# Adaptive-vector matmuls behind the first gate block, their weights in other buffers, and the sample's attention woven into two latent tiles

## The chip, the cores and the metric

One core of one Trainium2 chip runs the whole kernel in one launch. The metric is the device time of that launch in microseconds (us). The engines are named as the profile names them: PE (TensorE, matmuls; PEld is its weight load), DVE (VectorE), ACT (ScalarE), POOL (GpSimd) and SP (SyncE). SP and POOL issue nearly all DMAs.

## The reference, cut to what matters

One layer of a streaming encoder is computed for a prompt of 1024 rows and for a sample of 32 rows with 512 rows of cache; both share the weights. The model width is 1024.

```python
ada = jax.nn.silu(c) @ w_ada + b_ada            # 6 vectors of 1024 for each of the two groups
sh1, sc1, gt1, sh2, sc2, gt2 = split(ada, 6)
h = rms_norm(x, g_pre_mix) * (1 + sc1) + sh1
p = h @ w_in                                     # q-latent, kv-latent, rope key, SB q, k, v, gate A, gate B
# branch B ("SB", stick-breaking, strictly causal, 8 heads of 64):
z = einsum('bqhd,bshd->bhqs', q, k) * 0.125
sp = where(mask, softplus(z), 0); later = reversed_cumsum(sp) - sp
o_B = einsum(where(mask, exp(log_sigmoid(z) - later), 0), v)
# branch A: latent attention with softmax, from rms_norm(q-latent) and rms_norm(kv-latent)
merged = sigmoid(gate A) * (o_A @ w_proj_a) + sigmoid(gate B) * (o_B @ w_proj_b)
```

For the sample, branch B runs over 512 cached keys and values (`cache_sb_k`, `cache_sb_v`) and the 32 new ones. A projection, an output matrix and a convolutional feed-forward part follow; the change does not touch them.

## The kernel before, in words

A float32 product is made of three matmuls on a high and a low part of each factor (`mm3`, lines 72 to 74): ACT makes the high part of a weight tile (`wh`, line 65) and DVE the low part (`wl`, line 68) from the raw tile `wr`. The raw tiles come from the pool `W`, which has two buffers under the tag `wr`.

The stages that matter run one after the other:

- `stage_h` makes `h` and needs the first two adaptive vectors; `stage_qkv` makes SB's q, k and v and spills them to DRAM.
- `stage_sb` is SB attention of the prompt in four pairs of heads. For each pair the order of PE, ACT and DVE is written out by hand in the string `ORDER`. A token is a step and a tile: `S` scores (PE, lines 1117 and 1118, into one of three `s` banks), `a e l` Abs, Exp, Ln (ACT), `x c d` the softplus, the reversed running sum and the exponent (DVE; `d` is line 739 and is the last reader of the score bank), `E` Exp (ACT), `T h v` transposes and their two parts (PE, ACT, DVE), `V` the product with the values (PE, line 796), `o p` the output.
- Between these tokens stands filler work for PE, the token `f`: one step of the generator `gates`, which makes the 16 column tiles of the two gates. A tile `m` is 26 steps: two of `ada_step` (line 216, small matmuls on one tile of `w_ada` each), which make a part of the adaptive vectors 3 to 6, and three blocks of columns (`BLK`, eight `mm3` steps each). Each block and each `ada_step` fills one of two `mm` banks. The token `G` is ACT's copy of a block out of its bank (line 1046) and a DMA to DRAM; `D` and `Q` are DVE's steps on the adaptive vector (`D` is line 226: it adds the bank onto the tile `ada`, which a DMA on POOL has filled from `b_ada`, line 224). `W` and `w` split the next gate tile's weights.
- After the fourth pair the sample's branch B follows (`sb_sample`, for two pairs of heads each, `b` = 1 and then 0): transposes of the cached keys (line 984), scores (993, 995), weights (`sb_weights`, lines 806 to 817), transposes of them (940, 943) and the product with the values (954, 957). `stage_lat` makes the two tiles of the kv-latent (m = 3, 4, called x and y below; three blocks of 24 matmuls each), their sum of squares (`lat_sums`, line 1142) and then the q-latent.

What sets the order around the change: in `stage_sb` the hand-written order on PE, ACT and DVE; elsewhere, and for SP and POOL, a scheduler that builds the queues. Each queue runs in order, and an instruction that waits holds up all behind it.

Before, the two `ada_step` steps stand at the head of each tile, ahead of block 0. Their weights use the pool `W`, the same two `wr` buffers as the gate weights; only the first two tiles have places of their own (`ada_first`, in the pool of `stage_sb`). `b_ada` is loaded onto the tile `ada` when the vector begins. The sample's q, k, v (`sbd`) and caches are loaded into the pool `att`, which is opened after `stage_sb`, and the sample's steps and latent tiles stand in blocks: x, then the first half of `b` = 1, y, and so on, as the scheduler puts them.

Of the kernel before, what the change touches and what calls it, by code (L numbers as in the profile page):

```python
# [17 lines left out]
P = 128  # L18
# [26 lines left out]
class K:  # L45
    def __init__(self, tc, a, ctx):
        self.tc, self.nc, self.a, self.ctx = tc, tc.nc, a, ctx
        self.n = 0
        self.in_w = []

# [6 lines left out]
    def tl(self, pool, shape, dt=F32, tag=None, bufs=None):  # L57
        return pool.tile(shape, dt, tag=tag, name=self.nm(tag or "t"), bufs=bufs or self.BUFS.get(tag))
# [17 lines left out]

    def wload(self, parts):

        nc = self.nc
        raw = self.tl(self.W, [P, 1024], F32, "wr")  # L80
        for c0, n, src, k in parts:
            nc.sync.dma_start(raw[:, c0 : c0 + n].rearrange("p (k c) -> p k c", k=k), src)
        return raw
# [99 lines left out]
    def ada_prep(self, tp):  # L183
# [16 lines left out]
        self.cT = self.cp.tile([P, 8, 32], F32, name="cT")  # L200
        nc.vector.memset(self.cT, 0.0)
        nc.vector.tensor_copy(self.cT[:, :, 0:2], ps[:, 0:16].rearrange("p (j k) -> p k j", j=2))
        self.gtd = self.dr.tile([2, 2, D], F32, name="gtd")
        self.ada_todo = [(v, k) for v in range(2, 6) for k in range(KT)]

    def ada_step(self, n, pool, tp, late):
# [13 lines left out]
        if self.ada_todo[0][1] == 0:  # L220
            self.acc = self.tl(tp, [P, 256], F32, "ada")
            for j in range(4):
                c = v * D + j * 256
                nc.gpsimd.dma_start(self.acc[32 * j : 32 * j + 32], a["b_ada"][0, c : c + 256].partition_broadcast(32))
        acc = self.acc
        late.append(lambda: nc.vector.tensor_tensor(acc, acc, ps[:, :256], ALU.add))
        del self.ada_todo[:n]
        self.ada_sum = v if k == KT - 1 else None
# [196 lines left out]
    def stage_qkv(self):  # L425
# [248 lines left out]
        S2.1a x2.0b G f1 a2.1a d1.1 e2.1a c2.0b f1 f1 E1.1 f1 w l2.1a S2.1b f1 a2.1b x2.1a T1.1 e2.1b T1.0 d2.0b  # L674
        h1.1 c2.1a f1 h1.0 f1 l2.1b v1.1 S3.0a E2.0b v1.0 f1 a3.0a f1 k2.1a d2.1a G e3.0a x2.1b V1.1 E2.1a c2.1b
        l3.0a S3.0b V1.0 x3.0a a3.0b o1 f1 p1 T2.2 h2.2 e3.0b d2.1b f1 c3.0a f1 E2.1b f1 l3.0b v2.2 S3.1a k3.0a
        d3.0a T2.1 h2.1 a3.1a x3.0b E3.0a V2.2 f1 D c3.0b T2.0 e3.1a S3.1b h2.0 f1 v2.1 l3.1a f1 v2.0 a3.1b f1
        x3.1a W f1 d3.0b V2.1 c3.1a G V2.0 f1 w o2 S4.0 e3.1b E3.0b f1 a4.0 f1 l3.1b f1 p2 e4.0 k3.1a d3.1a l4.0
# [3 lines left out]
        f1 o3 c5.1 f1 a6.0b l6.0a e6.0b f1 p3 l6.0b d5.1 f2 x6.0b E5.1 V4.0 x6.0a D f1 o4 c6.0a S6.1a T5.1 p4  # L682
        a6.1a T5.0 k6.0a d6.0a h5.1 f1 c6.0b e6.1a f1 h5.0 v5.1 f1 E6.0a v5.0 S6.1b l6.1a f1 W f1 x6.1a d6.0b
        V5.1 V5.0 G c6.1a E6.0b a6.1b S7.0a w o5 f1 f1 e6.1b l6.1b a7.0a f1 k6.1a p5 e7.0a f1 d6.1a x6.1b E6.1a
        f1 c6.1b l7.0a S7.0b f1 x7.0a T6.2 a7.0b f1 d6.1b h6.2 c7.0a f1 E6.1b f1 G e7.0b S7.1a v6.2 f1 k7.0a
        d7.0a l7.0b T6.1 T6.0 a7.1a h6.1 V6.2 x7.0b c7.0b h6.0 S7.1b e7.1a f1 v6.1 E7.0a f1 v6.0 l7.1a f1 d7.0b
        a7.1b f1 x7.1a V6.1 E7.0b V6.0 e7.1b c7.1a f1 G o6 l7.1b f1 p6 k7.1a d7.1a x7.1b f1 f1 E7.1a f1 D c7.1b
        f2 T7.3 d7.1b T7.2 h7.3 f1 h7.2 E7.1b v7.3 f1 f1 v7.2 f1 V7.3 V7.2 G Q T7.1 f1 h7.1 v7.1 T7.0 f1 h7.0
        v7.0 f1 V7.1 f2 V7.0 f1 o7 f1 W p7 f2 w G f7 G
# [269 lines left out]

    def sb_sample(self, b):  # L960

        nc, a = self.nc, self.a
        os = self.osb
# [6 lines left out]
        hs = slice(4 * b, 4 * b + 4)  # L970
        ck = self.tl(self.At, [P, TP], F32, "A")
        with self.tc.issue_after(self.fetched):
            nc.sync.dma_start(ck.rearrange("p (t c) -> p t c", t=4),
                          a["cache_sb_k"][0, 0, :, hs].rearrange("(t p) h d -> p t (h d)", p=P))
        cv = self.tl(self.At, [P, BIG], F32, "big")
        with self.tc.issue_after(self.fetched):
            nc.sync.dma_start(cv[:, :TP].rearrange("p (t c) -> p t c", t=4),
                          a["cache_sb_v"][0, 0, :, hs].rearrange("(t p) h d -> p t (h d)", p=P))
        mm = [self.tl(self.At, [P, TP], F32, "A") for _ in range(2)]
        for pp in range(2):  # L980
# [5 lines left out]
            nc.vector.tensor_copy(mm[pp][:, PAST:KS], self.ksb[:, 2 * b + pp])  # L986
        pieces = []
# [10 lines left out]
        B = self.sb_weights(pieces[::-1], KS)  # L998

# [5 lines left out]
        def rest():  # L1005
            self.pv_sample(self.ptrans_sample(B), b, vals, os)
            for k in (2 * b, 2 * b + 1):
                nc.gpsimd.dma_start(self.obd[k][:, TP:T], os[:, k])

        return rest  # L1010

    def gates(self):
# [59 lines left out]
    def stage_sb(self):  # L1072
# [61 lines left out]
        for r, c in self.SB:  # L1134
            nc.sync.dma_start(x[r, c], self.sbd[r, c])
# [1435 lines left out]
```

## Time and profile before

| | us |
|---|---|
| median of 3 runs | 1716.11 (1715.53 to 1716.94) |
| the profiled execution's own time | 1719.25 |
| its span, first to last instruction | 1716.4 |
| PE busy in the span | 1663.4 |
| DVE busy | 1272.2 |
| ACT busy | 994.1 |
| POOL busy | 297.0 |

The profile is of one execution. Times in it count from the span's start. `stage_sb` lies from about 192 to 517 us, the sample's branch B and the latent tiles from about 517 to 565 us. In the rows of the timeline the columns are start, duration, engine, line, operation, output and inputs, shape, number of instructions, and in brackets how long the engine had idled and what released it. The granted clock (PEclk) is the share of full clock that PE was given in a stretch.

### The profile page before, as it was taken

Reading aid. Unit: us, or ns where it says so; the run is one execution under the profiler, and the core shown is the slowest. Engines: PE = TensorE matmul, PEld = TensorE weight load, DVE = VectorE, ACT = ScalarE, POOL = GpSimd, SP = SyncE. Lnnn points to the kernel's source line nnn. Section 1 sums busy time; section 2 is a strip of 40 time slices with the busy share of each in tenths; the row PEclk is TensorE's granted clock in tenths of the full one; section 3 lists DMA queues with packets and bytes.
Section 4 is the critical chain, followed back from the end, with each engine's and each line's share of the span. In section 5 each row is a group of like instructions: output and inputs, shape, how many; then the busy total and the mean of one; then the engine's idle time right before and its main releaser. Section 6 shows DMA issues by size and latency. Waiting matters only on the chain. (4 is left out here: it accounts for less than half of the span.)

```text
span 1716.4 us, 30275 instructions
## 1 busy us (share of the span) xinstructions
PE 1663.4 (97%) x11646; PEld 1516.1 (88%) x11646; DVE 1272.2 (74%) x2129; ACT 994.1 (58%) x1945; POOL 297.0 (17%) x569
## 2 busy tenths in 40 slices
PE   5999799999998999999999999999999999999997
PEld 3999799999998899988889789999999999977885
DVE  4865497979793488887776779887777787788456
ACT  4544487978783567777773476544444444544442
POOL 2113312111110131111100121211111122110013
PEclk8999899999999999999999999999999999999999
DMA  9345855565533331222174531423333333697643
GB/s 328 112 127 186 298 153 166 168 176 158 162 112 103 118 97 53 68 66 73 60 275 144 177 124 61 142 93 130 132 103 131 131 106 133 236 331 244 215 138 119
DMA packets 185728, 255.20 MB, mean 149 GB/s; under 512 B 14702, under 2 KB 125056, under 8 KB 185584
## 3 DMA queue, kind: packets, MB, share of 16 engines
q1 hardware_dynamic: 164944, 194.11, 36.3%
q0 software_dynamic: 20416, 59.08, 9.8%
q8 instruction: 91, 1.49, 0.4%
q14 instruction: 53, 0.43, 0.1%
q10 hardware_dynamic: 224, 0.09, 0.0%
HBM read 187.86 MB, written 64.57 MB: 147 GB/s over the span
## 5 line engine op out<-in xcount | busy, mean ns | idle before, releaser
L65 ACT ACTIVATE wh<-wr 128x1024 fp32r<-128x1024 f32 (+5 forms) x163 | 132.1, 820 | 222.8 <-PE s L2025 74.5
L68 DVE TENSOR_TENSOR wl<-wr,wh 128x1024 fp32r<-128x1024 f32 (+5 forms) x163 | 149.9, 928 | 84.4 <-ACT wh L65 84.3
L72 PE MATMUL mm<-hh,wh 128*128 128x352 f32 x456 | 154.7, 339 | 0.0
L73 PE MATMUL mm<-hl,wh 128*128 128x352 f32 x456 | 149.8, 329 | 0.1
L74 PE MATMUL mm<-hh,wl 128*128 128x352 f32 x456 | 149.2, 327 | 0.0
L2024 PE MATMUL mm<-T,wh 128*128 128x256 f32 (+1 forms) x376 | 108.0, 288 | 0.0
L2026 PE MATMUL mm<-T,wl 128*128 128x256 f32 (+1 forms) x376 | 107.0, 285 | 0.3 <-DVE wl L68 0.2
L2025 PE MATMUL mm<-T,wh 128*128 128x256 f32 (+1 forms) x376 | 106.7, 284 | 0.0
L2024 PE MATMUL s<-T,wh 128*128 128x256 f32 (+1 forms) x348 | 99.2, 285 | 0.0
L2026 PE MATMUL s<-T,wl 128*128 128x256 f32 (+1 forms) x348 | 99.1, 285 | 0.0
L2025 PE MATMUL s<-T,wh 128*128 128x256 f32 (+1 forms) x348 | 98.9, 284 | 0.0
L68 DVE TENSOR_TENSOR wl<-S,wh 128x1024 fp32r<-128x1024 f32 (+1 forms) x55 | 59.2, 1077 | 46.4 <-ACT wh L65 46.0
L72 PEld LDWEIGHTS mm<-hh,wh 128*128 128x128 f32 x456 | 87.5, 192 | 6.8 <-ACT o L768 3.3
L73 PEld LDWEIGHTS mm<-hl,wh 128*128 128x128 f32 x456 | 87.3, 191 | 2.9 <-DVE hl L312 1.4
L2165 DVE SCALAR_TENSOR_TENSOR u<-u,c,u 128x1058 f32<-128x1058 f32 x68 | 87.0, 1317 | 1.9 <-ACT u L2162 0.7
L74 PEld LDWEIGHTS mm<-hh,wl 128*128 128x128 f32 x456 | 87.0, 191 | 0.0
L782 PE MATMUL tr<-c,A 128*128 128x128 f32 x576 | 83.8, 274 | 0.9 <-ACT A L741 0.4
L65 ACT ACTIVATE wh<-S 128x1024 fp32r<-128x1024 f32 (+1 forms) x55 | 51.8, 943 | 50.9 <-PE s L2025 13.4
L2026 PE MATMUL tr<-T,wl 128*128 128x272 f32 (+1 forms) x272 | 77.7, 286 | 0.7 <-DVE wl L68 0.7
L2024 PE MATMUL tr<-T,wh 128*128 128x272 f32 (+1 forms) x272 | 77.7, 286 | 0.0
L2025 PE MATMUL tr<-T,wh 128*128 128x272 f32 (+1 forms) x272 | 77.3, 284 | 0.0
L68 DVE TENSOR_TENSOR PTl<-tr,PTh 128x512 fp32r<-128x512 f32 x96 | 64.6, 683 | 12.8 <-ACT PTh L65 12.5
(757 smaller groups left out, 5798.9 us busy)
## 6 DMA issues: line engine op xcount, KB each, us to landing
wr<-in_w_ada_dram SPq DMA_DIRECT2D x46, 512.0 KB, 5.8
wr<-in_w_up_dram SPq DMA_DIRECT2D x44, 512.0 KB, 4.1
dr<-in_w_down_dram SPq DMA_DIRECT2D x43, 512.0 KB, 5.8
wr<-in_w_in_dram SPq DMA_DIRECT2D x33, 512.0 KB, 4.7
wr<-gdn SPq DMA_DIRECT2D x30, 512.0 KB, 5.0
gdn<-u POOLq DMA_DIRECT2D x23, 512.0 KB, 5.1
gd<-nat POOLq DMA_DIRECT2D x48, 176.0 KB, 3.0
t<-gd SPq DMA_DIRECT2D x16, 528.0 KB, 5.3
```

Source lines behind the costliest of these rows:

```text
L65: self.nc.scalar.activation(out, in_, AF.Identity, scale=scale)
L68: return self.nc.vector.tensor_tensor(out, full, hi.bitcast(F32), ALU.subtract)
L72: m(ps, lh, rh, start=start, stop=False)
L73: m(ps, lh, rl, start=False, stop=False)
L74: self.pe = m(ps, ll, rh, start=False, stop=stop).ins
L782: self.nc.tensor.transpose(tr[:, (2 * s + q) * P : (2 * s + q + 1) * P], at[q][:, b * P : b * P + P], self.idt)
L2024: m(ps[:, :n], w[0][:, k], x[0][:, k, c], start=first and k == 0, stop=False, skip_group_check=True)
L2025: m(ps[:, :n], w[0][:, k], x[1][:, k, c], start=False, stop=False, skip_group_check=True)
L2026: i = m(ps[:, :n], w[1][:, k], x[0][:, k, c], start=False, stop=k == 3, skip_group_check=True)
L2165: nc.vector.scalar_tensor_tensor(y, u[:, w : w + YW], self.cvT[:, w, cc : cc + 1], y, ALU.mult, ALU.add)
```

## The change

1. In each gate tile the two `ada_step` steps move behind block 0. `ORDER` has new places for `G`, `D` and `Q`, and its first filler steps come as `f2`; the numbers of steps between the other tokens stay. The turning of a finished vector moves from block 0 to block 1.
2. The adaptive weights leave `wr`. Tile m's two are loaded by `ada_fetch` as soon as tile m-1's steps are written, into the tag `A` of the pool `att` (five buffers), which is now opened at the head of `stage_sb`. The first two take two of the five `A` buffers of `stage_sb`'s own pool, as before. `PTh`, `PTl`, `nat` and `o` of the later stages move to a second pool (`att2`).
3. `b_ada` of the first of these vectors goes to a constant tile `acc`, by four DMAs written in `stage_qkv`.
4. From the first `queries` to the end of the sample's part, all loads of SP go through `load`, which ties each behind the one written before it.
5. The sample's `sbd` and its caches of `b` = 1 are loaded from within the last gate tile (`sample_load(1)`), those of `b` = 0 in the first step of `b` = 1.
6. In `stage_lat` PE's order is written out: block 0 of x, transposes of `b` = 1, block 1, scores of `b` = 1, block 2, block 0 of y, transposes of the weights, block 1, values, transposes of `b` = 0, block 2, scores of `b` = 0. What is left of `b` = 0 goes to the scheduler.

```diff
+    def load(self, out, src):
+        with self.tc.issue_after(self.sent) if self.sent is not None else ExitStack():
+            ins = self.nc.sync.dma_start(out, src).ins
+        self.wlast = ins
+        if self.sent is not None:
+            self.sent = ins
...
+    def ada_fetch(self, n, pool):
+        for v, k in self.ada_todo[:n]:
+            self.ada_w.append(self.tl(pool, [P, D], F32, "A"))
+            self.load(self.ada_w[-1], self.a["w_ada"][0, k * P : (k + 1) * P, v * D : (v + 1) * D])
...
     def ada_step(self, n, pool, tp, late):
...
-            w = self.ada_first.pop(0) if self.ada_first else self.tl(pool, [P, D], F32, "wr")
-            with self.tc.issue_after(self.begun):
-                nc.sync.dma_start(w, a["w_ada"][0, k * P : (k + 1) * P, v * D : (v + 1) * D])
+            w = self.ada_w.pop(0)
...
         del self.ada_todo[:n]
+        self.ada_fetch(n, pool)
...
             pair(i, ta, tb, *U[i % 2 * 2 : i % 2 * 2 + 2])
-            if i == 1:
+            if i == 0:
+                self.ada_bias(2)
+            elif i == 1:
...
     ORDER = """
-        S0.0 S0.1 a0.0 S1.0 a0.1 e0.0 e0.1 l0.0 f1 f1 l0.1 x0.0 a1.0 x0.1 f1 c0.1 c0.0 e1.0 f1 l1.0 f1 d0.0 d0.1
-        E0.0 f1 x1.0 c1.0 E0.1 f1 D S1.1 S2.0a a1.1 T0.0 d1.0 f1 a2.0a h0.0 v0.0 f1 e2.0a f1 e1.1 S2.0b l2.0a G
-        f1 f1 l1.1 x2.0a V0.0 E1.0 c2.0a f1 a2.0b o0 f1 x1.1 e2.0b f1 W p0 f1 k2.0a d2.0a l2.0b f1 c1.1 E2.0a f1
+        S0.0 S0.1 a0.0 S1.0 a0.1 e0.0 e0.1 l0.0 f2 l0.1 x0.0 a1.0 x0.1 f1 c0.1 c0.0 e1.0 f1 l1.0 f1 d0.0 d0.1
+        E0.0 f1 x1.0 c1.0 E0.1 f1 S1.1 S2.0a a1.1 T0.0 d1.0 f1 G a2.0a h0.0 v0.0 f1 e2.0a f1 e1.1 S2.0b l2.0a D
+        f2 l1.1 x2.0a V0.0 E1.0 c2.0a f1 a2.0b o0 f1 x1.1 e2.0b f1 W p0 f1 k2.0a d2.0a l2.0b f1 c1.1 E2.0a f1
...
             for m in range(16):
                 wh, wl = w.pop(0)
-                yield from self.ada_step(2, self.W, self.Sp, ada)
                 for b, (c0, n) in enumerate(self.BLK):
...
-                    if b == 0 and self.ada_sum is not None:
+                    if b == 1 and self.ada_sum is not None:
                         ada.append(self.ada_turn())
                     yield
+                    if b == 0:
+                        yield from self.ada_step(2, self.sm2, self.Sp, ada)
+                        if m == 15:
+                            self.sample_load(1)
...
-        fc = latent(3, 1, lp, "lt")
-        self.sample_rest()
-        rest = self.sb_sample(0)
-        fc += latent(4, 1, lp, "lt")
-        rest()
+        fc = []
+        with self.tc.manual_schedule(engines={mybir.EngineType.PE}):
+            x, y = latent(3), latent(4)
+            s1 = self.sb_sample(1)
+            for g in (x, s1, x, s1, x, y, s1, y, s1):
+                next(g)
+            s0 = self.sb_sample(0)
+            for g in (s0, y, s0):
+                next(g)
+        list(s0)
+        self.sent = None
```

More of the change, by code (lines that the diff above doesn't have):

```diff
@@ L219, in ada_step @@
                 yield
-        if self.ada_todo[0][1] == 0:
+        if v > 2 and self.ada_todo[0][1] == 0:
             self.acc = self.tl(tp, [P, 256], F32, "ada")
-            for j in range(4):
-                c = v * D + j * 256
-                nc.gpsimd.dma_start(self.acc[32 * j : 32 * j + 32], a["b_ada"][0, c : c + 256].partition_broadcast(32))
+            self.ada_bias(v)
         acc = self.acc
@@ L1106, in stage_sb @@
         self.diagonals(S)
-        self.ada_first = [self.tl(S, [P, D], F32, "A") for _ in range(2)]
         for _ in range(3):
@@ L1110, in stage_sb @@
         first(0)
-        self.begun = queries(0, 0)
+        self.sm2 = self.tc.alloc_tile_pool(name="att", bufs=2, reuse_waits="tile")
+        self.sent = self.wlast
+        queries(0, 0)
+        self.ada_w = []
+        self.ada_fetch(2, S)
         values(0, 0)
```

102 lines of the change are left out of this document (56 added, 46 removed).

## The prediction

> **What bounds the kernel.** I read the page first: PE is busy nearly always, so time can be won only where PE idles or runs at a lower clock. Then the windows, in stretches that I chose by the stages.
>
> ```profile
> PE 1663.4 (97%) x11646; PEld 1516.1 (88%) x11646; DVE 1272.2 (74%) x2129; ACT 994.1 (58%) x1945; POOL 297.0 (17%) x569
> ```
>
> ```profile
> 193.00:218.20 25.20, 15.31 (x78) 13.27 (x79) 11.53 (x24) 11.55 (x28) 8.54 (x18) 0.73 0.80 302
> 218.20:266.00 47.80, 47.74 (x336) 44.52 (x336) 46.32 (x81) 43.58 (x96) 6.63 (x12) 1.00 0.55 155
> 266.00:517.50 251.50, 249.89 (x1777) 232.22 (x1776) 211.61 (x370) 199.84 (x437) 42.97 (x80) 1.00 0.55 157
> 528.80:536.30 7.50, 5.12 (x25) 3.49 (x24) 1.54 (x7) 3.69 (x9) 0.00 (x0) 0.77 0.67 195
> 544.20:552.00 7.80, 5.72 (x39) 4.45 (x40) 2.31 (x8) 3.24 (x9) 1.08 (x2) 1.00 0.23 59
> ```
>
> The columns are stretch, its length, busy time of PE, PEld, DVE, ACT and POOL, then PE's granted clock and the DMA's share. In the head of SB attention (193 to 218.2) PE idles 25.20 - 15.31 = 9.9 us and has 0.73 of its clock. In the 299 us after that it idles 0.06 + 1.61 = 1.7 us. In the sample's part it idles 7.50 - 5.12 = 2.4 us at 0.77 of the clock, and 7.80 - 5.72 = 2.1 us. The change touches little else, so these three stretches are what it can win.
>
> **The head of SB attention.** The timeline and the waits of PE give the holes.
>
> ```profile
> PE mm L216 <- ACT A L725: 4.9, 1, 4.9
> PE s L1117 <- DVE A L739: 4.0, 2, 3.7
> PE mm L216 <- DMA wr<-in_w_ada_dram: 0.8, 3, 0.4
> ```
>
> ```profile
> 192.57 0.34 PE L1118 MATMUL s<-KL,Q 128*128 128x384 f32 x1
> 197.78 1.08 PE L216 MATMUL mm<-A,cT 128*32 128x256 f32 x8 [4.87 <-ACT A L725]
> 198.32 0.62 DVE L739 TENSOR_TENSOR A<-s,A 128x128 f32<-128x128 f32 x2
> 199.44 0.96 DVE L734 TENSOR_TENSOR_SCAN A<-reset,A 128x384 f32<-128x384 bf16 x1
> 200.23 1.08 PE L216 MATMUL mm<-A,cT 128*32 128x256 f32 x8 [1.37 <-DMA A<-in_w_ada_dram]
> 201.70 0.49 PE L73 MATMUL mm<-hl,wh 128*128 128x352 f32 x1
> 201.99 0.49 PE L74 MATMUL mm<-hh,wl 128*128 128x352 f32 x1
> ...
> 210.98 0.42 DVE L226 TENSOR_TENSOR ada<-ada,mm 128x256 f32<-128x256 f32 x1 [10.58 <-DMA ada<-in_b_ada_dram]
> 211.92 0.64 PE L1117 MATMUL s<-KH,Q 128*128 128x320 f32 x1 [3.75 <-DVE A L739]
> 217.53 0.32 PE L74 MATMUL mm<-hh,wl 128*128 128x352 f32 x1
> 217.69 0.32 PE L72 MATMUL mm<-hh,wh 128*128 128x352 f32 x1
> 218.18 0.34 PE L1117 MATMUL s<-KH,Q 128*128 128x384 f32 x1
> 218.31 0.68 DVE L739 TENSOR_TENSOR A<-s,A 128x512 f32<-128x512 f32 x1
> 220.45 0.33 PE L1117 MATMUL s<-KH,Q 128*128 128x384 f32 x1
> ```
>
> PE has its first three scores by 192.9 and then meets the first `ada_step`, whose weights are still in flight: 4.87 us of idling. (The row names ACT as releaser; no step of PE's there needs ACT's line 725, but the next step waits for the same kind of load, so I take it to be the DMA.) The second costs 1.37. Meanwhile `D` stands in DVE's queue ahead of everything else, and the DMA of `b_ada` sits on POOL behind the spills: DVE stops for 10.58 us, the score banks aren't freed, and PE idles 3.75 more. The clock falls: consecutive matmuls start 0.29 us apart (201.70 to 201.99) where they start 0.16 apart later (217.53 to 217.69).
>
> From 192.9 to the score at 218.18 (token `S2.1a`) PE takes 25.3 us. Both orders have 18 filler steps there, two adaptive and 16 of gate matmuls. At full clock the 16 take 16 x 3 x 0.16 = 7.7 us, the two adaptive ones at most 2 x 1.08 / 2 = 1.1 (their rows were taken at half clock), and `S1.1`, `S2.0a`, `S2.0b`, `T0.0` and `V0.0` some 1.8 by like rows (0.3 to 0.5 each): 10.6 us. So 14.7 us are lost, the upper bound.
>
> After the change: seven gate steps follow the three scores at once. Their weights were split in the stage before, so PE works to 192.9 + 7 x 0.48 = 196.3. Then it needs `S1.1`, whose bank `d0.0` frees. That chain on ACT and DVE is not moved; it ended with the first half of the row at 198.32, at 198.63. So 2.4 us of idling stay, and the clock will probably fall after them, as it does at 531 below, for some 2.2 us. The adaptive step comes at about 201, where before its weights were there at 197.78 and 200.23; in the built program its two loads stand ahead of the second head's `Q`, which waits for the stage before, so they start earlier and are no longer late. `D` waits no longer: `b_ada` has been there since the start. By PE's path the gain at `S2.1a` is 14.7 - 2.4 - 2.2 = 10.1 us. By DVE's path: the stop of 10.58 us goes, but DVE is now ahead of its feeders and waits some 2 us (an estimate: `D` for the adaptive matmuls at low clock, the second row's Abs for a score tile that is now a buffer of the first row, since the adaptive weights hold two of five until then). That is 8.6 us; at 218.99 (218.31 + 0.68) DVE had freed its bank 1.5 us before PE took it at 220.45, so up to 10.1. Behind 218.2 DVE is 97% busy and PE never idles, so there is little room for DVE to be later. I take 9.5, bounds 5 (DVE's waits doubled and nothing to spare) and 14.7.
>
> At one point the rule and the trace differ. A gap of 2.46 us (528.83 to 531.29, below) brought matmuls 0.30 us apart for the next 4.5 us: half the clock, some 2.2 us lost. The Trainium skill, page "TensorE: Matmul & The Clock Gate", section "Why this matters for your kernels", asks for gaps of no more than about 3 us, with an idle window of about 3.4 us before the clock drops. By that rule the gap of 2.4 us would cost no clock. The measured gap decides against it.
>
> **The rest of SB attention.** Of 12 remaining gate tiles and 3 pairs little is to be won: 1.7 us. What could be lost is a new wait for an `mm` bank: `G` empties block 0's bank, and block 1 takes it two adaptive steps later, 1.0 us at 0.5 each and often a score more.
>
> ```profile
> 218.37 0.45 ACT L1046 COPY nat<-mm 128x352 f32<-128x352 f32 x1 [0.49 <-PE mm L74]
> ```
>
> The copy takes 0.45 us. Before, block 2's bank and the next block 0 stood in just this relation (`G` two adaptive steps ahead), and 251.5 us show 1.6 us of idling. I take 0, range 3 lost to 1.5 won. SP's loads in written order wait for PE or DVE only at the place where they are written, and that is a good part of a gate tile or of a pair ahead of their use: 0. The loads that waited for `wr` do not bind now either: PE's waits above name the adaptive ones with 0.8 us in all.
>
> **The sample and the latent tiles.**
>
> ```profile
> 525.31 0.42 SPq L973 DMA_DIRECT2D A<-in_cache_sb_k_dram  x1
> 528.83 0.32 PE L74 MATMUL mm<-hh,wl 128*128 128x352 f32 x1
> 531.29 1.06 PE L984 MATMUL tr<-c,A 128*128 128x128 f32 x8 [2.14 <-DMA A<-in_cache_sb_k_dram]
> 534.60 0.40 ACT L806 ACTIVATE A<-s 128x272 f32<-128x272 f32 x1 [1.57 <-PE s L993]
> 535.77 0.49 PE L73 MATMUL s<-hl,wh 128*128 128x352 f32 x1
> 536.07 0.39 PE L74 MATMUL s<-hh,wl 128*128 128x352 f32 x1
> 540.74 0.41 ACT L817 ACTIVATE A<-A 128x272 f32<-128x272 f32 x1
> 543.52 1.06 ACT L65 ACTIVATE wh<-wr 128x1024 fp32r<-128x1024 f32 x1 [2.37 <-PE s L73]
> ```
>
> ```profile
> PE pv L954 <- ACT A L941: 1.3, 1, 1.3
> PE pv L954 <- DVE A L957: 0.6, 1, 0.6
> ```
>
> The keys are asked for at 525.31, when PE is nearly done with x: 2.14 us of waiting, then the low clock. Later PE waits 1.3 us for the copy of the transposed weights and 0.6 for the one `pv` bank. Sum with the two short waits: 2.4 + 2.1 + 2.2 of clock = 6.7 us, all that is to be had. After the change the keys are asked for within the last gate tile, at least a whole block of x ahead. The weights of `b` = 1 take 540.74 + 0.41 - 534.60 = 6.6 us on ACT and DVE, behind block 2 of x and block 0 of y (2 x 24 x 0.16 = 7.7 us): covered, by 1 us. The copies are covered by a block. What stays or comes new: 0.6 for the `pv` bank; y's weights, split by ACT (1.06) and DVE only behind the Exp and Ln of the sample, so that block 0 of y waits some 0.6 for its low part; the sum of squares, which stands 3.3 us of matmuls behind the last scores while ACT has a weight split (1.06), y's last copy and square and the sample's chain ahead of it, some 0.8; and the values of `b` = 0, some 1.0. That is 3.0, each new one an estimate from these durations. Gain 6.7 - 3.0 = 3.7, bounds 1 and 6.
>
> **The start.** The four DMAs of `b_ada` are written in `stage_qkv`, but nothing holds them there: in the built program they stand on POOL right behind the load of line 388, ahead of the first norms.
>
> ```profile
> 4.05 0.58 POOL L388 DMA_DIRECT2D c<-in_k_sel_dram  x1
> ...
> 11.54 0.19 POOL L97 TENSOR_SCALAR rv<-ss 128x1 f32<-128x1 f32 x1 [1.19 <-ACT jk L105]
> 11.81 3.04 POOL L98 TENSOR_TENSOR rs<-rv,c 128x1 f32<-128x1 f32 x4
> 21.15 0.64 PE L270 MATMUL s<-wr,cT 128*32 128x256 f32 x8 [0.75 <-DMA wr<-in_w_ada_dram]
> ```
>
> Four issues of 0.58 us end at about 7.0, and the last of the four norms waits for ACT until 11.54: hidden by 4.5 us. The start is bound by its loads (21.15), so their 128 KB, at the 302 GB/s of the first windows row, may cost 0.4 us. I take 0.3, range 0 to 2 should the fourth, which waits for an earlier load's semaphore, be late.
>
> **The sum.** -9.5 + 0 - 3.7 + 0.3 = -12.9 us on the profiled execution: 1719.25 - 12.9 = 1706.4. That execution lies 3.1 us above the median of the three runs; the same loss from 1716.1 gives **1703.2**.
>
> **Rivals.**
> - *DVE and ACT set the pace of the head*: PE runs ahead on gate steps and then idles for the score banks. For it: DVE is 97% busy from 218 to 266. Against: PE never idles there. The head gives 5, the sample 2.5: 1709. Chance 0.16.
> - *The clock stays up* in the 2.4 us gap (the rule above): 2.2 more, 1701.0; with fewer new waits in the sample, 1699. Chance 0.15. Against it stands the gap of 2.46 us.
> - *The change does not win*: what PE gains is given back at the next fixed point. For it: PE's head start needs loads that share the DMA with the spills (0.80 busy in the head). Nothing later is tied to the clock, so I see no such point; 1716. Chance 0.03.
> - *Slower by bank waits*: block 1 of a tile waits for `G` of block 0, in 16 tiles. ACT is 79% busy (199.84 of 251.50), so a copy can stand behind a row of Exp or Ln. Each us by which the copy comes later than its 1.0 us costs 16 us in all; from 0.8 us too late in each tile the 12.9 us are gone. At 1.2 us too late: 19 - 13 = 6 us slower, 1722. Against it: the same relation held before with 1.6 us of idling in 251.5. Chance 0.09.
> - The forecast has the rest, 0.57.
>
> **Range and chances.** The forecast with its bounds lies at 1699 to 1708; the two smaller-gain and larger-gain rivals widen it to 1698 to 1710.5, which leaves the last two rivals and some tails out, under 0.2. A difference of 0.2%, 3.4 us, is about what a measurement of this kernel tells from none. Faster by more: 0.57 + 0.16 + 0.15 = 0.88; within: 0.03; slower: 0.09.
>
> **What would show it.** Right: in the waits of PE the first `ada_step` row and the 3.75 us on DVE's line 739 are gone, a wait of about 2.4 us for `S1.1` stands in their place with a low clock for 4 us behind it; DVE's 10.58 us are gone; `S2.1a` comes near 208.5; the wait for the keys is gone; SB attention's middle stays under 3 us of idling. Wrong: PE waits on line 72 for ACT's line 1046; DMA waits on the adaptive tiles of the second gate tile, whose buffers lie over spilled tiles; a head that ends beyond 213; or a shift in the stages behind 580 us.

## The result, and the profile after

| | before | after |
|---|---|---|
| median of the runs (four of each, side by side) | 1715.82 us (1715.22 to 1716.94) | 1706.84 us (1702.90 to 1708.63) |
| ratio, with its 95% interval | | 0.9944 (0.9926 to 0.9962) |
| profiled execution: time, span | 1719.25, 1716.4 | 1706.82, 1704.7 |

The change takes 9.0 us off the median; a second measurement of the same kernel gave 0.9947 (0.9934 to 0.9961). The forecast was 1703.2 (1698.0 to 1710.5), so the total came out inside it. Its parts did less well: what SB attention lost lies outside its bounds, what the sample won lies just past its upper bound, and the two errors go in opposite directions.

I cut both traces at the same four instructions of PE (first score of SB attention, score `S4.0`, last score, first matmul with `wk`) and take the differences. Each stage then holds the same work of PE. The profiled execution of before lay 3.4 us above the median of its runs and that of after on its median, so the differences of the stages add up to 11.7 us of span where the medians show 9.0.

| stage, us | before | after | after, run again |
|---|---|---|---|
| start and QKV, to the first score | 191.84 | 193.01 | 193.24 |
| first score to `S4.0` | 42.85 | 34.76 | 36.01 |
| `S4.0` to the last score | 266.24 | 268.52 | 268.58 |
| last score to the first `wk` matmul | 89.06 | 82.97 | 83.17 |
| the rest | 1126.4 | 1125.4 | 1124.9 |

The windows of these stages, before and then after. The columns are stretch, length, busy time of PE, PEld, DVE, ACT and POOL (with their instructions), PE's granted clock, the DMA's share and its GB/s. The first two rows of each kernel meet at `S2.1a`, the end of the head in the prediction.

```profile
191.84:218.18 26.34, 16.35 (x86) 13.99 (x85) 12.67 (x25) 11.97 (x30) 9.43 (x20) 0.74 0.81 305
218.18:234.69 16.51, 16.51 (x119) 14.98 (x119) 16.10 (x28) 14.85 (x32) 1.66 (x3) 1.00 0.57 156
234.69:500.93 266.24, 264.57 (x1872) 246.29 (x1871) 229.98 (x404) 218.09 (x482) 44.08 (x81) 1.00 0.56 161
500.93:589.99 89.06, 84.25 (x552) 78.26 (x550) 42.82 (x87) 43.85 (x94) 10.82 (x19) 0.98 0.36 102
```

```profile
193.01:208.92 15.91, 13.42 (x86) 11.81 (x84) 12.00 (x24) 10.20 (x27) 9.01 (x20) 0.89 1.06 362
208.92:227.77 18.85, 17.05 (x119) 15.08 (x118) 16.65 (x28) 16.60 (x36) 2.53 (x5) 1.00 0.88 239
227.77:496.29 268.52, 266.55 (x1871) 246.40 (x1871) 231.58 (x406) 219.13 (x482) 41.39 (x76) 1.00 0.57 168
496.29:579.26 82.97, 81.91 (x552) 76.45 (x550) 42.08 (x86) 43.39 (x94) 10.85 (x19) 1.00 0.30 87
```

So the head wins 26.34 - 15.91 = 10.4 us, and 18.85 - 16.51 = 2.3 are given back at once, 268.52 - 266.24 = 2.3 more in the long rest. In that rest PE has the same instructions (1872 and 1871 records) and idles 1.97 us against 1.67, but its busy time is 2.0 us longer at the same clock of 1.00. In the profile the ends of matmuls are modelled; I take it that short waits between two of them count as busy. The idle column shows 0.3 of the 2.3 us. The waits of DVE in the same stretch show more (after; times as in the other rows of waits):

```profile
DVE c L259 <- PE tr L256: 2.5, 3, 0.8
DVE ptd L71 <- ACT ptd L68: 2.4, 3, 0.8
```

The first is the turning of a finished vector (`Q`), which now waits for PE's transposes; before, no such row is there. The second, DVE behind ACT's copy of the transposed tile `ptd`, was 1.1 before.

The waits of PE after (engine, line, releaser: us in total, times, longest). The rows of the prediction on the adaptive step, on the keys and on the copied weights are gone; 5.4 us on the scores (4.0 before) and 0.6 on the `pv` bank remain, and the wait for the start's weights is 4.6 where it was 3.7.

```profile
PE s L1154 <- DVE A L760: 5.4, 7, 2.5
PE s L289 <- DMA wr<-in_w_ada_dram: 4.6, 5, 2.9
PE pv L975 <- DVE A L978: 0.6, 1, 0.6
```

The timeline of the head after: PE's gate steps run to 197.12, the wait for `S1.1`, matmuls 0.30 us apart behind it, a wait of ACT for a score tile that PE's transposes still read, with DVE behind it, and then a wait that the prediction did not have.

```profile
187.98 1.90 SPq L83 DMA_DIRECT2D wr<-in_w_in_dram  x1
197.12 0.32 PE L77 MATMUL mm<-hh,wl 128*128 128x352 f32 x1
199.94 0.64 PE L1154 MATMUL s<-KH,Q 128*128 128x512 f32 x1 [2.49 <-DVE A L760]
202.06 0.60 ACT L742 ACTIVATE A<-s 128x512 f32<-128x512 f32 x1 [1.50 <-PE tr L803]
202.27 0.49 PE L76 MATMUL mm<-hl,wh 128*128 128x352 f32 x1
202.57 0.49 PE L77 MATMUL mm<-hh,wl 128*128 128x352 f32 x1
204.31 0.56 DVE L71 TENSOR_TENSOR ptd<-tr,ptd 128x384 fp32r<-128x384 f32 x1 [2.14 <-ACT ptd L68]
210.12 1.06 ACT L68 ACTIVATE wh<-wr 128x1024 fp32r<-128x1024 f32 x1 [2.59 <-DMA wr<-in_w_in_dram]
211.57 0.49 DVE L748 SCALAR_TENSOR_TENSOR A<-s,A 128x320 f32<-128x320 f32 x1 [2.06 <-ACT A L746]
212.71 0.44 PE L1154 MATMUL s<-KH,Q 128*128 128x384 f32 x1 [1.36 <-DVE A L760]
```

The second gate tile's weights, asked for at 187.98, are there at 210.1; the DMA's share was 1.06 in the first row above. `W` (the hi part of these weights) stands on ACT ahead of the next score row's work: ACT waits 2.59 us, DVE for ACT 2.06, PE for DVE 1.36.

The sample after: the keys are asked for 14 us before PE wants them, and the transposes follow block 0 of x without a gap. One wait of 0.57 is left.

```profile
506.26 0.37 SPq L83 DMA_DIRECT2D A<-in_cache_sb_k_dram  x1
520.61 0.32 PE L77 MATMUL mm<-hh,wl 128*128 128x352 f32 x1
520.77 0.49 PE L1011 MATMUL tr<-c,A 128*128 128x128 f32 x3
540.98 0.29 PE L975 MATMUL pv<-A,big 128*128 128x64 f32 x1 [0.57 <-DVE A L978]
```

### The profile page after: what moved, and what is told of

The parts are those of the page before. It is cut to its first block, busy times and chain, and to the rows that moved or that the text cites. A ratio compares the mean times of both kernels' runs of the same rounds, so it can differ in the third digit from the quotient of the medians.

```text
span 1704.7 us, 30268 instructions
## 1 busy us (share of the span) xinstructions
PE 1660.8 (97%) x11646; PEld 1512.1 (89%) x11646; DVE 1272.9 (75%) x2129; ACT 993.6 (58%) x1945; POOL 292.8 (17%) x569
```

## The experiments

The theory at first: PE's path sets the head, the start costs 1.2 us, the late weights and the new places of `G` cost what is given back. The rival throughout: DVE (fed by ACT) sets the pace, and PE's gains are only shifted. The version in which each edit is made is named; lines are cut to the core.

### `bias_late`: the DMAs of `b_ada` later on POOL

```diff
-        nc.gpsimd.dma_start(self.l2d, lf)
+        l2 = nc.gpsimd.dma_start(self.l2d, lf).ins
...
-                self.ada_bias(2)
+                with self.tc.issue_after(l2):
+                    self.ada_bias(2)
```

> The changed kernel, with the four DMAs of b_ada held behind the store of l2d on POOL, in the middle of the QKV stage; that also puts PE's first transposes and adaptive matmuls back into the order that they had before the change. Theory: the early DMAs delay the first norms, and so the start costs 1.2 us. Then the first score comes at 191.8 to 192.0 instead of 193.01, the whole span is 1.1 us shorter (1703.6), and D still waits for nothing. Rival: the 1.2 us are a chance of the start's loads; then the first score stays near 193.0 and the time where it is.

The start's result, the first transposes of the adaptive sum, came 0.86 us sooner than after. In the changed kernel POOL waits ahead of the third and fourth DMA, with the first norms behind them (POOL and PE after; then PE of this run).

```profile
7.31 0.50 POOL L226 DMA_DIRECT2D acc<-in_b_ada_dram  x1 [1.71 <-DMA mk<-in_k_mask_dram]
8.43 0.50 POOL L226 DMA_DIRECT2D acc<-in_b_ada_dram  x1 [0.62 <-DMA xs<-in_x_sample_dram]
23.04 0.44 PE L294 MATMUL s<-c,ada 128*128 128x128 f32 x2 [0.55 <-DVE ada L291]
```

```profile
22.18 0.44 PE L294 MATMUL s<-c,ada 128*128 128x128 f32 x2 [0.55 <-DVE ada L291]
```

Over all profiles that row lies at 22.1 to 22.3 without the early DMAs and at 22.7 to 23.1 with them: the start costs 0.4 to 1.0 us. But the first score came at 192.69, not 191.9. Between the two rows the same code took 168.3 to 170.5 us in the profiles (that of `unsent`, which delays the first score itself, left out), so what is left of the 1.17 is not shown to be the change's.

What PE itself waits for in the start is the adaptive weights, and their first use comes 0.40 us later (before, then after):

```profile
11.72 1.08 PE L270 MATMUL s<-wr,cT 128*32 128x256 f32 x8 [2.21 <-DMA wr<-in_w_ada_dram]
12.12 1.08 PE L289 MATMUL s<-wr,cT 128*32 128x256 f32 x8 [2.88 <-DMA wr<-in_w_ada_dram]
```

So the four DMAs may cost by their load on the DMA or by holding up POOL; no run separates the two. Time 1705.88 (0.9938, 0.9921 to 0.9955): not told from the change's.

### `raw_free`: the second tile's weights outside SP's written order

```diff
+                        sent, self.sent = self.sent, self.sent if m else None
                         raw.append(self.wload(...))
+                        self.sent = self.sent if m else sent
```

> The changed kernel, with the load of the second gate tile's weights taken out of SP's written order, so that it goes out before the QKV stage ends, as it did before the change. Theory: the 2.59 us that ACT waits for these weights at 210.12 come from the written order; they go, and with them PE's 1.36 us ahead of the score S2.1b, which comes 18.3 us behind the first score instead of 19.70; the end is 1.4 us earlier. Rival: DVE sets the pace there in any case; S2.1b comes sooner, but at the last score of pair 0 less than 0.4 us of it is left.

The waits for the weights went and `S2.1b` came 18.87 behind the first score instead of 19.70. `S4.0` came at 34.82 (34.76 after): the rival was right. Another wait stood behind the first, ACT's for the buffer of a gate block's copy whose store had not left, and DVE's for ACT (timeline of this run). Time 1707.49 (0.9945, 0.9930 to 0.9960).

```profile
215.73 0.45 ACT L1082 COPY nat<-mm 128x352 f32<-128x352 f32 x1 [1.73 <-DMA gd<-nat]
217.56 0.62 DVE L748 SCALAR_TENSOR_TENSOR A<-s,A 128x448 f32<-128x448 f32 x1 [1.15 <-ACT A L746]
```

### `gap_filled`: three more filler steps ahead of `S1.1`

```diff
-E0.0 f1 x1.0 c1.0 E0.1 f1 S1.1 S2.0a a1.1 T0.0 d1.0 f1 G a2.0a h0.0 v0.0 f1 e2.0a f1 e1.1 S2.0b l2.0a D
+E0.0 f1 x1.0 c1.0 E0.1 f4 S1.1 S2.0a a1.1 T0.0 d1.0 G a2.0a h0.0 v0.0 e2.0a e1.1 S2.0b l2.0a D
```

> The changed kernel, with three more filler steps (the eighth gate step and the two adaptive ones) ahead of the score S1.1 in place of behind it, in every pair. PE's path: its wait of 2.49 us for S1.1 shrinks to some 1.0, and if a gap of that length leaves the clock up (one of 1.27 us did before the change), the score S2.1a comes 12.2 us behind the first score instead of 15.9, and the end is 3.7 us earlier. If the clock falls all the same, S2.1a comes some 15.5 behind the first score and the end moves by under 0.5. Rival: ACT and DVE set the pace of the head; then S2.1a may come sooner, but S2.1b and what follows stay within 1 us of where they were.

The wait for `S1.1` shrank to 1.02 as worked out, but two others took its place, and the clock fell all the same (PE's waits, then the windows around them).

```profile
198.15 0.47 PE L1154 MATMUL s<-KH,Q 128*128 128x512 f32 x1 [1.02 <-DVE A L760]
200.44 0.42 PE L1154 MATMUL s<-KH,Q 128*128 128x320 f32 x1 [0.96 <-DVE A L760]
201.81 0.43 PE L75 MATMUL mm<-hh,wh 128*128 128x352 f32 x1 [0.81 <-ACT nat L1080]
```

```profile
198.00:202.00 4.00, 2.08 (x10) 1.52 (x11) 2.31 (x5) 2.02 (x6) 1.98 (x5) 1.00 1.07 408
202.00:206.00 4.00, 4.00 (x17) 4.00 (x17) 3.11 (x7) 3.71 (x10) 2.15 (x6) 0.57 0.86 256
```

`S2.1a` came later (16.56 against 15.91), `S4.0` 1.4 us earlier (33.37, hardly more than two runs of one kernel differ there, see `after_again`), and in the pairs behind it, where no gap had to be filled, the moved steps cost 273.64 - 268.52 = 5.1 us. So filling PE's one gap does not bring `S2.1a` forward: PE then waits for DVE and ACT, and the clock falls behind these waits. Time 1708.58 (0.9956, 0.9941 to 0.9971).

### `g_behind`: two copies `G` behind the ACT work that DVE waits for

```diff
-T0.0 d1.0 f1 G a2.0a h0.0 v0.0 f1
+T0.0 d1.0 f1 a2.0a h0.0 v0.0 G f1
...
-l3.1a f1 G v2.0 a3.1b f1
+l3.1a f1 v2.0 a3.1b G f1
```

> The changed kernel, with two G of every pair (the copies of a gate block's bank on ACT) moved behind the ACT work that DVE needs next: the first behind h0.0 and v0.0, the other behind a3.1b. Theory: against the kernel before, SB attention loses some 0.9 us in each pair because these copies stand ahead of what DVE waits for, and DVE, 97% busy, never makes it up. Then the last score comes 1.5 to 3 us earlier behind the first (301.8 to 300.3 instead of 303.3 us), and the end as much. Rival: DVE's own work or the waits of PE make the loss; then the last score stays within 0.5 us, or comes later where the next block now waits for its bank.

The stretch from `S4.0` to the last score took 267.13 us instead of 268.52: 1.4 of the 2.3 us come back. The last score came 302.13 behind the first, 1.2 us earlier, just short of the expected band. Time 1706.26 (0.9939, 0.9924 to 0.9954): 1.4 us are too little to be seen there. DVE's 2.4 us behind ACT's copies of `ptd` are gone in this run; its 2.5 us on `Q` are not. The places of `G` are part of what SB attention lost, not all of it; `Q` may be another part, but no run moves it alone.

### `before_bias`: the kernel before with `b_ada` loaded early, nothing else

```diff
+        self.acc = self.cp.tile([P, 256], F32, name="acc")
...
+            if i == 0:
+                self.ada_bias(2)
...
-        if self.ada_todo[0][1] == 0:
+        if v > 2 and self.ada_todo[0][1] == 0:
```

> The kernel before with one part of the change alone: the first four DMAs of b_ada are issued in the QKV stage into a tile of their own, so that the first D no longer waits for them; order, adaptive weights and loads are as before. The score S4.0 came 42.85 us behind the first score before the change and 34.76 behind it. If DVE's pace decides the head, nearly all of these 8.1 us come from this part: DVE's wait of 10.58 us goes, PE's waits of 4.87 and 1.37 us for the adaptive weights stay, and S4.0 comes at 35 to 37. If PE's path decides, as the prediction's 10.1 us were worked out, those two waits and the clock behind them keep S4.0 at 38 to 40. The end is earlier than before by what S4.0 gains, less up to 0.7 for the start.

PE's two waits for adaptive weights stayed (5.00 and 1.48 us; PE's row names the DMA for both, as the prediction took it), and still `S4.0` came at 37.75, between the two bands: 5.1 of the 8.1 us. Windows of this run, first score to `S4.0` and from there to the last score:

```profile
193.27:231.02 37.75, 31.27 (x203) 27.68 (x201) 28.82 (x52) 26.63 (x62) 11.10 (x23) 0.86 0.81 280
231.02:496.33 265.31, 264.48 (x1871) 246.48 (x1871) 229.86 (x404) 218.25 (x482) 42.09 (x77) 1.00 0.57 161
```

DVE is busy 28.82 us to `S4.0`; before it was 12.67 + 16.10 = 28.8, after 12.00 + 16.65 = 28.7. What differs is its idle time: 14.1 us before, 8.9 here, 6.1 after. ACT's busy time is as constant (26.8, 26.6, 26.8), so these sums alone don't say which engine leads. The waits say more: the stop of 10.58 us on `b_ada` is gone, but PE, late by its adaptive weights, now holds ACT for 7.24 us at `S1.1`, and ACT holds DVE (timeline of this run).

```profile
208.07 0.93 ACT L727 ACTIVATE A<-s 128x512 f32<-128x512 f32 x2 [7.24 <-PE s L1124]
209.42 0.56 DVE L68 TENSOR_TENSOR ptd<-tr,ptd 128x384 fp32r<-128x384 f32 x1 [5.48 <-ACT ptd L65]
```

So both paths of the prediction reach `S4.0`: DVE's stop for the larger part, PE's adaptive waits for the rest. From the first to the last score this one part of the change needs 303.06 us and the whole change 303.28: in SB attention as a whole the other parts add up to nothing. Time 0.9974 (0.9960 to 0.9988) of before, 4.5 us less.

### `ada_first`: the changed kernel with the order of before

```diff
                 wh, wl = w.pop(0)
+                yield from self.ada_step(2, self.sm2, self.Sp, ada)
...
-                    if b == 0:
-                        yield from self.ada_step(2, self.sm2, self.Sp, ada)
...
+(the order string and the block of the turn as before)
```

> The changed kernel with the adaptive visits back ahead of a tile's first gate block, and with the order written out for SB attention as it was before; loads, buffers, b_ada and the sample's part stay changed. PE's path: the two adaptive weights, asked for at 186.3 and some 8 us on their way, hold PE for 2 to 4 us right behind the first three scores, and S4.0 comes 37 to 39 us behind the first score instead of 34.8. DVE's pace: S4.0 stays within 1 us of 34.8. Behind S4.0 the theory that the new places of G on ACT cost SB attention 1.4 to 2.3 us expects the last score 266 to 267 us behind S4.0 (266.2 before the change) instead of 268.5; the rival, that the new buffers or loads cost it, expects 268.5 again.

Neither theory: `S4.0` came at 40.31, the time is 1719.67 us, slower than before (1.0024, 1.0011 to 1.0038). `S2.1a` came at 14.13, sooner than with the new order, and the adaptive weights cost 0.95 us. Then PE stood for 7.85 us behind DVE, DVE behind ACT, and ACT behind the second tile's weights. SP's queue and ACT tell why:

```profile
187.68 0.58 SPq L83 DMA_DIRECT2D V<-vd  x1
206.16 1.11 SPq L83 DMA_DIRECT2D A<-in_w_ada_dram  x2
207.34 0.42 SPq L83 DMA_DIRECT2D wr<-in_w_in_dram  x1
215.22 1.06 ACT L68 ACTIVATE wh<-wr 128x1024 fp32r<-128x1024 f32 x1 [9.22 <-DMA wr<-in_w_in_dram]
```

With the visit ahead of block 0, the next two adaptive loads are written ahead of the tile's `wr`, and they cannot go before 206 (nor do they after the change: 206.57). In the written order `wr` stands behind them. ACT has such a wait of 2.9 to 4.0 us in each later pair too, so the 277.08 us behind `S4.0` say nothing on the places of `G`.

### `sample_late` and `lat_old`: the two halves of the sample's part

`sample_late` holds the loads back, `lat_old` takes the order of before; both on the changed kernel.

```diff
-                        if m == 15:
-                            self.sample_load(1)
...
+        if b:
+            nc.scalar.copy(self.ck[:, 0:1], self.last_g[:, 0:1])
...
             x, y = latent(3), latent(4)
+            self.sample_load(1)
```

```diff
-            for g in (x, s1, x, s1, x, y, s1, y, s1):
+        for g in (s1, s1, x, x, x, s1, s1):
...
-            for g in (s0, y, s0):
+        for g in (s0, s0, y, y, y):
```

> The changed kernel with the sample's loads (its Q, K and V rows, its keys and values for b = 1) held back to where the last gate block's copy is done: a copy of one column on ACT writes into the tile of the keys first, and the load waits for it. The order of the latent tiles and the sample stays changed. From the last score of SB attention to the first matmul with wk it took 89.07 us before and 83.0 to 84.7 in the runs of the change so far. Theory: about two thirds of that gain is the early load (a wait of some 2 us and a low clock of 2.2 us behind it); then it takes 87 to 88.5 here, with a wait of PE for the keys ahead of the transposes. Rival: the order alone covers it; then 83 to 85.

> The changed kernel with the sample and the latent tiles written in their order of before (scores of b = 1, all of x, its weights and values, scores of b = 0, all of y, then the rest), without an order written out for PE; the loads stay early. From the last score to the first matmul with wk: 89.07 us before, 83.0 to 84.7 with the change. Theory: the order is worth the smaller part, the 1.3 and 0.6 us that PE waited for the copied weights and the pv bank and part of the 1.5 us of short waits; then 85 to 87 here. Rival: the early load is all of the gain; then 83 to 84.7.

From the last score to `wk`: 86.74 with late loads, 83.60 with the old order; 89.06 before; 82.5 to 84.7 in all runs with both parts. So `lat_old` came out as its rival had it, `sample_late` between its two bands. With early loads the order is worth nothing that can be seen; with late loads it is worth 89.06 - 86.74 = 2.3 us, or more by what the clock took below. They cover the same waits, and the early load alone is enough. The wait for the keys in `sample_late` (timeline):

```profile
516.35 0.39 SPq L83 DMA_DIRECT2D A<-in_cache_sb_k_dram  x1
521.11 1.07 PE L1013 MATMUL tr<-c,A 128*128 128x128 f32 x8 [1.70 <-DMA A<-in_cache_sb_k_dram]
541.36 1.08 PE L975 MATMUL pv<-A,big 128*128 128x64 f32 x8 [0.57 <-DVE A L978]
```

Behind those 1.70 us the clock stayed up. It fell 20 us later, behind the wait of 0.57 us for the `pv` bank. Three more runs show such a fall there (`bias_late`, `g_behind`, `first_rawtop_more`); they took 84.1 to 84.7 us for this stretch, where the others with both parts took 82.5 to 83.4. So some 1.5 of the 86.74 us are chance, by this estimate. Times: 0.9959 (0.9949 to 0.9969) and 0.9946 (0.9927 to 0.9965).

### `first_rawtop`: the old order, and the tile's next weights written ahead of the visit

On `ada_first`; the load leaves its place in block 0, and the first one stands outside SP's written order, as in `raw_free`:

```diff
                 wh, wl = w.pop(0)
+                sent, self.sent = self.sent, self.sent if m else None
+                raw.append(self.wload(...))
+                self.sent = self.sent if m else sent
                 yield from self.ada_step(2, self.sm2, self.Sp, ada)
```

> The changed kernel with the adaptive visits and the written-out order of before (ahead of a tile's first gate block), and with a tile's next weights written ahead of the adaptive visit, the first of them outside SP's written order. So it is the change without its new order, and without the load that queued behind adaptive weights whose buffers were not free. Theory: the new order is worth nothing by itself; it only kept the next tile's weights ahead of those adaptive loads, and behind the head it costs 2 to 3 us. Then PE's wait of 7.85 us in the run with the old order goes, S4.0 comes 31 to 34 us behind the first score (34.76 with the change), the last score 265 to 267 behind S4.0 (268.5 with the change), so 297 to 301 in all instead of 303.3, and the span is 2 to 6 us shorter than the change's. Rival: with the old order the adaptive weights of later tiles come late in each pair; then the last score comes at 303 or later and the time is no better than the change's.

The theory held: `S4.0` at 32.79, the last score 264.95 behind it, the time 1701.98 (0.9924, 0.9910 to 0.9938), by the ratios 3 to 4 us under the change's. Only the span fell by more than the 2 to 6 us expected. Windows, first score to `S4.0` and on to the last score:

```profile
191.25:224.04 32.79, 29.18 (x203) 25.61 (x201) 28.46 (x52) 25.57 (x60) 10.97 (x23) 1.00 0.95 305
224.04:488.99 264.95, 263.99 (x1872) 246.59 (x1871) 229.98 (x405) 219.03 (x484) 41.93 (x77) 1.00 0.58 169
```

The profiled span, 1697.0, is 7.7 us under that of after; 5.5 of it is SB attention (303.28 - 297.74), 1.8 an earlier first score, which the edit does not explain. So the new order by itself costs some 2 us in the head and 3.6 behind it; against `raw_free`, which frees the same load, it is 34.82 - 32.79 = 2.0 and 268.68 - 264.95 = 3.7. The part in the head is mostly the clock: it stayed at 1.00 behind a wait of 1.67 us for `S1.1`, where 0.95 over the 34.76 us of after is a loss of 1.7. Behind `S4.0` the two waits of DVE, on `Q` and for `ptd`, are gone from its list. What the new order did for the change was to keep `wr` ahead of the adaptive loads.

### `unsent`: no written order for SP's loads

```diff
-        self.sent = self.wlast
+        self.sent = None
```

> The changed kernel without SP's written order: its loads are not held behind one another, and their place in the queue is the scheduler's. In the built program the weights of the third gate tile then stand ahead of the first head's Q, K and V, and wait for a buffer that is free only when the QKV stage's last weights are split, at about 191; the sample's values stand within the first pair's loads. Theory: the written order is needed, not free: Q comes some 9 us later than at 180.0, and the first score at 196 to 200 instead of 191.2 to 193.4; the end is later by as much, less what the second tile's weights gain. Rival, the price of nothing in the prediction: the first score stays at 191 to 193.5 and the time within 2 us.

The theory was right, its size too small: the first score came at 202.73, where 196 to 200 was expected. SP stands at 173.49 with the third tile's weights (18.89 us) and asks for Q at 192.47; the first score waits 9.48 us for the lower part of Q, and the time can't be told from that of before (0.9992, 0.9983 to 1.0001).

```profile
173.49 18.89 SPq L83 DMA_DIRECT2D wr<-in_w_in_dram  x3
192.47 0.55 SPq L83 DMA_DIRECT2D Q<-qh  x1
202.73 0.58 PE L1154 MATMUL s<-KH,Q 128*128 128x256 f32 x1 [9.48 <-DMA Q<-ql]
```

From `S4.0` to the last score this run took 268.61 us. With the new order it is 268.4 to 268.7 in seven runs, whether loads are held or free; with the old order 264.3 to 266.2 in the four runs whose `wr` was not late. The 2 to 4 us behind `S4.0` are the new order's, not the loads'.

### `after_again` and `first_rawtop_more`: the change once more, and two more edits on `first_rawtop`

The second adds the hold of `bias_late` and a third buffer for `G`'s copies.

```diff
-("nat", 512, 2)):
+("nat", 512, 3)):
...
-                g = self.tl(self.At, [P, 512], F32, "nat")
+                g = self.tl(self.At, [P, 512], F32, "nat", 3)
```

> The changed kernel once more, unaltered, beside the version below: how far its stages move from one execution to the next. The first score came at 191.2 to 193.4 us over the runs with the same code ahead of it; if that is chance of the start and the QKV stage, it lies in that span again, while the ada result of the start comes at 22.7 to 23.1, the last score 303.1 to 303.7 behind the first, and the first wk matmul 83.0 to 84.7 behind the last score. If one of these is off by more than 1 us, the terms read from single profiles are no better than that.

> The version with the old order and the tile's next weights written ahead of the adaptive visit, and two more edits: b_ada held behind the store of l2d on POOL, and a third buffer for the copies of the gate blocks, for which ACT waited 2.41 us at 213.78 (DMA gd<-nat) and PE 1.21 and 0.68 behind it. Theory: the ada result of the start comes at 22.2 instead of 22.7 to 23.1, S4.0 comes 30.5 to 31.5 behind the first score instead of 32.79, and the last score at 295.5 to 297; the time is 1 to 2.5 us under that of the version without them. Rival: behind the wait for the buffer stands one for the DMA itself, saturated until 222 us; then S4.0 stays at 32 to 33 and the time within 1 us.

The change again: first score 193.24, ada result 22.91, last score 304.59 behind the first (0.9 above its band, all of it ahead of `S4.0`), 83.17 to `wk`. In this execution the clock fell behind a second wait, of 1.51 us at 213.12 (0.72 in the 6 us behind it); the like waits of 1.36 (after) and 1.60 us (`g_behind`) were passed at 1.00. So terms of under 1.5 us in the head can't be read from single profiles.

`first_rawtop_more`: 1701.61 us, 0.9920 (0.9906 to 0.9933), just clear of the change's interval in the same comparison (0.9934 to 0.9961), no different from `first_rawtop`. The ada result came at 22.08, and the wait for the buffer went; then PE waited for the next loads (timeline), and `S4.0` stayed at 33.78: the rival.

```profile
194.21 0.64 PE L236 MATMUL mm<-A,cT 128*32 128x256 f32 x8 [1.08 <-DMA A<-in_w_ada_dram]
196.60 0.64 PE L236 MATMUL mm<-A,cT 128*32 128x256 f32 x8 [1.75 <-DMA A<-in_w_ada_dram]
205.68 0.60 PE L818 MATMUL pv<-ptd,V 128*128 128x256 f32 x3 [2.05 <-DMA V<-vd]
```

## Why the prediction was right, and where it was not

- **The head, -9.5 (5 to 14.7).** Measured -10.4 at `S2.1a`, near the 10.1 of PE's path: a wait of 2.49 us for `S1.1` (predicted 2.4), matmuls 0.30 us apart behind it, `S2.1a` at 208.92 (predicted near 208.5, though the first score came 1.17 later). The adaptive weights and `D` no longer wait. All this was read rightly; only the low clock, put at 2.2 us, was sized too high: a clock of 0.72 over 6 us is 1.7. But `S2.1a` was the wrong place to stop: six scores later, at `S4.0`, 8.1 us are left (6.8 in the second run). The prediction's other path, DVE's, was put at 8.6. Of its two waits the one on the score tile came (ACT 1.50 us, DVE 2.14 behind it), the one on `D` did not. That 8.6 and 8.1 lie so close is partly luck: the 2.06 us behind the late weights were not in it, nor was a wait of DVE for ACT's `o`, 1.71 us before, that went. `before_bias` shows that `S4.0` hangs on both paths: with DVE's stop alone taken away 5.1 of the 8.1 us come.
- **The rest of SB attention, 0 (3 lost to 1.5 won).** 4.6 us were lost, outside the bounds: 2.3 between `S2.1a` and `S4.0`, 2.3 behind. Behind `S4.0` the step that failed is the price of the new order. It was priced only as a wait for a bank on PE (the slower rival; PE's waits of after have no such row), not as ACT's and PE's work standing ahead of what DVE needs. `G` on ACT is one part (`g_behind` gives 1.4 us back), the turning of the vectors probably another (2.5 us of DVE's waits), and with the old order the whole loss is gone (`first_rawtop`). Up to `S4.0` the step "SP's loads in written order: 0" overlooked that the second tile's weights would be used 22 us after their issue, with a full DMA, and hold ACT for 2.59 us. But `raw_free` takes this wait away and leaves `S4.0` where it was, since another wait stands behind it; what the 2.3 us there hang on stays open. The sign that was offered, under 3 us of idling, came true with 1.97 and showed nothing, since the loss stands in PE's busy time.
- **The sample, -3.7 (1 to 6).** Measured -6.1. The keys' wait, the low clock behind it and the 1.3 us went as predicted, and the 0.6 for the `pv` bank stayed (0.57). The mis-sized term is the three new waits of 0.6, 0.8 and 1.0 us: PE idles 1.06 us in the whole stretch (4.81 before), 0.5 beside the `pv` bank. The written order of PE, which the sum leaned on for the covers, was not needed for it (`lat_old`).
- **The start, +0.3 (0 to 2).** 0.4 to 1.0 us. The risk that was named came: POOL waited ahead of the third DMA (1.71 us) and the fourth (0.62). So that the four issues end at about 7.0 was wrong (8.9), and the first norms on POOL stand behind them. But the load on the DMA, put at 0.4, can have cost it as well; which of the two did is not shown.
- **The sum.** On the profiles: 10.4 won, 4.6 lost, 6.1 won, 1.2 lost at the first score, 1.0 won behind 580, together 11.7 of the span where 12.9 was forecast. The last term is not shown to be the change's: that stretch takes 1124.0 to 1126.7 us over all profiles. That the total fits is luck in this much: an under-rated gain (the sample) and an under-rated loss (the rest of SB attention) cancelled.
- **The rivals.** That DVE and ACT set the pace was half right: it decides what of the head is kept. The clock that stays up in the 2.4 us gap did not happen. That the head's win is given back behind it was given 0.03, and happened to 4.6 of 10.4 us.

## What to carry to other kernels

Measure a stage's gain where the engine that is densest behind it has caught up, not where the freed engine first shows it: count that engine's busy and idle time in the stretch, and look at what its idle time waits for. Compare stretches by equal instructions, since short waits hide in PE's busy time. When loads are tied into a written order, ask of each what it now stands behind, and when that one's buffer comes free; here the old order with one load written further ahead beat the new order.

## What the runs showed of the hardware

The clock: seven runs with the new order have a wait of PE of 2.49 to 2.61 us for `S1.1` (2.49 in after). In the 6 us from its end the granted clock was 0.72 in six of them and 0.76 in `raw_free`; 0.72 over 6 us is 3.4 us at half clock. The wait of 2.14 us for the keys before (the gap of 2.46 in the prediction, which counts from start to start) was followed by 0.72 too. Shorter waits went both ways. Behind 1.51 (`after_again`), 1.78 (`before_bias`) and 1.83 us (`ada_first`) the clock was 0.72; behind 1.67 (`first_rawtop`), 1.70 (`sample_late`), 1.87 (`gap_filled`) and 2.05 us (`first_rawtop_more`) it was 1.00. Even the wait of 0.57 us for the `pv` bank was followed by 0.72 in four runs and by 1.00 in the others. Several waits close together went both ways as well: 1.02, 0.96 and 0.81 us within 4 us brought the clock to 0.57 (`gap_filled`), 1.08 and 1.75 us within 4 us left it up (`first_rawtop_more`). The Trainium skill, page "TensorE: Matmul & The Clock Gate", section "Why this matters for your kernels", allows gaps of up to about 3 us; the waits of 2.5 us and the shorter ones with 0.72 do not agree with it. What decides between like gaps, these runs do not show.

The DMA: with its share at 1.0 or above, a load of 512 KB took over 20 us from issue (187.98) to use (210.12). Freeing one buffer or moving one load there brought out the next one's wait (`raw_free`, `first_rawtop_more`).
